# L2 pooling on one core: two 63 KB input slots and pairwise adds in place of four 32 KB slots and a reduce

## The chip, the cores and the metric

The kernel runs on one core of one Trainium2 chip. The metric is the device time of one execution in microseconds (us). The kernel before takes 395.71 us (median of six runs, 395.51 to 395.85). Times below are medians of several executions of the same kernel; all runs with more than one execution are in the fast state, at full clock.

## The reference, cut to what matters

```python
x = randn(32, 256, 4096)  # float32, 134 MB
window = np.abs(x[:, :, 4*i:4*i+4]) ** 2.0          # p == 2, kernel_size == 4
result[:, :, i] = np.mean(window, axis=-1) ** 0.5   # (32, 256, 1024), 34 MB
```

Each input element is read once, squared, summed in fours, and a root is taken of each sum. The data is 33.5 million elements, 262144 for each of the 128 partitions. Nothing is used twice, so 167.8 MB must go through the DMA engines in any version.

## The kernel before

Four input slots of 8192 elements (32 KB) per partition. Three loads are always asked for ahead of the one in use. Four slots make a group with one output tile, which one store sends. ACT (ScalarE) squares in place, DVE (VectorE) reduces in fours, ACT takes the root one chunk later. The last two stores before the final one are held back so that they run while the last load is worked on.

```python
W, CH, GROUP, LAST = 8192, 4096, 4, 1
in_pool  = tile_pool(bufs=4)      # 4 x 32 KB
out_pool = tile_pool(bufs=2)      # 2 x 32 KB
...
for i in range(n):
    if i + 3 < n:
        load(i + 3)                                   # SyncE (SP) queue
    ...
    for c in range(0, W, CH):
        xh = xts[i][:, c:c + CH]
        nc.scalar.activation(out=xh, in_=xh, func=Square)                     # L108
        nc.vector.tensor_reduce(out=ots[gi][:, at:at + CH // k],              # L112
            in_=xh.rearrange("p (n j) -> p n j", j=k), axis=X, op=add)
        if pending is not None:
            root(*pending)        # Sqrt on ACT, L87; store on the ACT queue when a group is done
        pending = (i, c)
root(*pending)
for gi in sorted(held):
    nc.sync.dma_start(out=out_block(gi), in_=ots[gi])
```

## Time and profile before

| | before |
|---|---|
| time, us | 395.71 |
| span of the profiled run, us | 393.7 |
| DVE busy | 72% |
| ACT busy | 75% |
| moved | 167.79 MB, 426 GB/s over the span |

These lines are from the profile page of the kernel before. First the busy share of each engine; then the span in 40 equal slices, with the DMA engines' busy share in tenths and the rate in GB/s; then the packets; then the chain of waits that ended last; then groups of instructions (busy us, mean ns of one | idle before them and what ended it).

```profile
span 393.7 us, 357 instructions
...
DVE 282.8 (72%) x64; ACT 294.7 (75%) x130; POOL 0.2 (0%) x4
...
DMA  8999998999999999999999999999999999999997
GB/s 350 446 430 426 426 426 373 449 446 430 433 426 426 426 430 453 440 430 433 426 426 426 426 449 443 427 433 430 426 426 426 443 446 433 430 433 426 426 435 314
DMA packets 5906, 167.79 MB, mean 426 GB/s; under 512 B 656, under 2 KB 656, under 8 KB 656
...
DMA 72%; ACT 17%; DVE 9%; SPq 0%; issue 0%; ACTq 0%
...
L112 DVE TENSOR_REDUCE ot<-xt 128x1024 f32<-128x4096 f32 x64 | 282.8, 4420 | 103.4 <-ACT xt L108 102.6
L108 ACT ACTIVATE xt<-xt 128x4096 f32<-128x4096 f32 x64 | 230.9, 3610 | 87.6 <-DMA xt<-in_x_dram 85.0
```

The DMA row is full and both compute engines sit idle for about a quarter of the time, so the DMA engines bound the kernel.

The trace also holds every DMA packet with its start and duration. A packet here is one descriptor: one contiguous piece for one partition. Median durations are 309 ns for 8 KB, 912 ns for 24 KB and 1213 ns for 32 KB, which is about 0.03675 ns per byte plus 9 ns.

### The profile page before, as it was taken

What the parts mean: (1) busy time and instruction counts of PE and PEld (TensorE: products, weight loads), DVE (VectorE), ACT (ScalarE), POOL (GpSimd) and SP (SyncE); (2) the same over time, 40 slices, a digit from 0 to 9 for tenths busy, and PEclk for the clock granted to TensorE, in tenths of its full rate; (3) what the DMA queues carried; (4) which work ended last, traced back from release to release, by engine and by line L of the source; (5) the groups of instructions that cost most, each with busy time, mean ns of one, the idle gap of its engine ahead of it and who ended that gap; (6) DMA issues with size and microseconds to landing.
All of it is one profiled execution on the core that took longest, in us unless ns stands there. A gap on an engine that the chain in (4) does not pass through costs nothing.

```text
span 393.7 us, 357 instructions
## 1 busy us (share of the span) xinstructions
DVE 282.8 (72%) x64; ACT 294.7 (75%) x130; POOL 0.2 (0%) x4
## 2 busy tenths in 40 slices
DVE  0399996739976399764988559866598846999992
ACT  1699987469883798828988189863998819999981
POOL 0000000000000000000000000000000000000000
DMA  8999998999999999999999999999999999999997
GB/s 350 446 430 426 426 426 373 449 446 430 433 426 426 426 430 453 440 430 433 426 426 426 426 449 443 427 433 430 426 426 426 443 446 433 430 433 426 426 435 314
DMA packets 5906, 167.79 MB, mean 426 GB/s; under 512 B 656, under 2 KB 656, under 8 KB 656
## 3 DMA queue, kind: packets, MB, share of 16 engines
q1 hardware_dynamic: 4896, 141.56, 83.9%
q10 hardware_dynamic: 1008, 26.21, 15.5%
q14 instruction: 2, 0.02, 0.0%
HBM read 134.22 MB, written 33.55 MB: 426 GB/s over the span
## 4 chain that ended last, share of the span: by engine, by line
DMA 72%; ACT 17%; DVE 9%; SPq 0%; issue 0%; ACTq 0%
DMA xt<-in_x_dram 72%; ACT xt L108 14%; DVE ot L112 9%; ACT ot L87 2%; SPq L79 0%; ACTq L108 0%
## 5 line engine op out<-in xcount | busy, mean ns | idle before, releaser
L112 DVE TENSOR_REDUCE ot<-xt 128x1024 f32<-128x4096 f32 x64 | 282.8, 4420 | 103.4 <-ACT xt L108 102.6
L108 ACT ACTIVATE xt<-xt 128x4096 f32<-128x4096 f32 x64 | 230.9, 3610 | 87.6 <-DMA xt<-in_x_dram 85.0
L87 ACT ACTIVATE ot<-ot 128x1024 f32<-128x1024 f32 x64 | 67.0, 1047 | 4.2 <-DVE ot L112 3.4
L108 ACT ACT_TABLE_LOAD x1 | 1.3, 1283 | 0.7 <-PEq L139 0.7
L87 ACT ACT_TABLE_LOAD x1 | 1.3, 1283 | 0.0
L139 POOL MEMSET const-uint8-127<- 128x1 uint8 x1 | 0.1, 102 | 0.0
L139 POOL MEMSET const-bfloat16-1.0<- 128x1 bf16 x1 | 0.1, 101 | 0.0
L139 POOL MEMSET const-float32-0.0<- 128x1 f32 x1 | 0.1, 98 | 0.2 <-issue 0.2
L139 POOL MEMSET const-float32-1.0<- 128x1 f32 x1 | 0.1, 98 | 0.0
## 6 DMA issues: line engine op xcount, KB each, us to landing
xt<-in_x_dram SPq DMA_DIRECT2D x32, 4096.0 KB, 35.9
out_dram<-ot ACTq DMA_DIRECT2D x6, 4096.0 KB, 23.2
out_dram<-ot SPq DMA_DIRECT2D x1, 4096.0 KB, 34.1
out_dram<-ot SPq DMA_DIRECT2D x1, 3072.0 KB, 12.3
out_dram<-ot ACTq DMA_DIRECT2D x1, 1024.0 KB, 5.6
```

The source lines that it names most:

```text
L87: nc.scalar.activation(out=o, in_=o, func=mybir.ActivationFunctionType.Sqrt, scale=1.0 / k,)
L108: nc.scalar.activation(out=xh, in_=xh, func=mybir.ActivationFunctionType.Square,)
L112: nc.vector.tensor_reduce(out=ots[gi][:, at:at + CH // k], in_=xh.rearrange("p (n j) -> p n j", j=k), axis=mybir.AxisListType.X, op=mybir. ...
L139: nc = _bacc.Bacc("TRN2", target_bir_lowering=False, num_devices=1)
```

## The change

The intent is to give DMA larger descriptors (63 KB instead of 32 KB per partition), with two slots instead of four (126 KB in place of 128 KB), and to shorten the arithmetic so that two slots suffice: two pairwise adds in place of the reduce, and DVE takes an eighth of the squares from ACT. A tail of four loads of 31.5 KB and one of 16 KB per partition ends the kernel.

```diff
-    W = 8192
-    CH = 4096
-    GROUP = 4
+    CH = 4032
+    W = 4 * CH            # 63 KB
+    H = W // 2
+    BIG = 14
+    END = total - BIG * W - 4 * H      # 4096
-    in_pool = ... bufs=4 ; out_pool = ... bufs=2 ; last_pool = ... bufs=1
+    x_pool = ... bufs=2  ; o_pool = ... bufs=2   ; s_pool = ... bufs=2
...
+    def add1(v):          # first adds, L70: columns 0,1 plus 2,3 of each four
+        vv = v.rearrange("p (n j) -> p n j", j=4)
+        nc.vector.tensor_tensor(out=s..., in0=vv[:, :, 0:2], in1=vv[:, :, 2:4], op=Alu.add)
+    def add2(o, s):       # second adds, L78
+        sv = s.rearrange("p (n j) -> p n j", j=2)
+        nc.vector.tensor_tensor(out=o, in0=sv[:, :, 0], in1=sv[:, :, 1], op=Alu.add)
...
+    for i in range(BIG):
+        square_dve(c[3][:, 0:CH // 2])                        # L61
+        square_act(c[0]); square_act(c[1]); square_act(c[2])  # L58
+        square_act(c[3][:, CH // 2:CH])
+        s0 = add1(c[0]); add2(o[0], s0)
+        s1 = add1(c[1]); add2(o[1], s1)
+        s2 = add1(c[2]); s3 = add1(c[3]); add2(o[2], s2); add2(o[3], s3)
+        if i + 2 < BIG:        load(i + 2)                    # L85, SP queue
+        elif i + 2 == BIG:     load_tail((0, 1))              # L103
+        else:                  load_tail((2, 3))
+        root(ot[:, base:base + 2 * CH // k]); root(...)       # L64
+        if i % 2 == 1 and i < BIG - 1:
+            nc.scalar.dma_start(out=block(of, ...), in_=ot)   # L140, ACT queue
...
+    for j in range(5):
+        if j == 2:
+            last_x = load_tail((4,))      # takes the slot of small loads 0 and 1
+        ... per chunk: square_act, add1, add2, root of the chunk before
+    nc.sync.dma_start(..., in_=ot_pair)   # L165, 4.1 MB, held back
+    nc.sync.dma_start(..., in_=ot_three)  # L166, 3.1 MB
+    nc.sync.dma_start(..., in_=ot_two)    # L167, 1.56 MB
```

(The repeated cuts are marked; calls on one line are separate lines in the kernel.)

More of the change, by code (lines that the diff above doesn't have):

```diff
@@ L33 @@
     fp32 = mybir.dt.float32
+    Act = mybir.ActivationFunctionType
+    Alu = mybir.AluOpType
     xf = x.rearrange("b c l -> (b c l)")
@@ L36 @@
     total = xf.shape[0] // P
-    W = 8192
-    CH = 4096
-    GROUP = 4
-    LAST = 1
-    n = total // W
-    assert n * W == total
-    groups = []
-    i = 0
-    while i < n - LAST:
-        g = min(GROUP, n - LAST - i)
-        groups.append((i, g))
-        i += g
-    groups += [(j, 1) for j in range(n - LAST, n)]
-    held = {len(groups) - 1 - LAST - j for j in range(2)}
-    group_of = {}
-    for gi, (first, g) in enumerate(groups):
-        for j in range(g):
-            group_of[first + j] = gi
@@ L59 @@
-    in_pool = ctx.enter_context(tc.tile_pool(name="in_pool", bufs=4))
-    out_pool = ctx.enter_context(tc.tile_pool(name="out_pool", bufs=2))
-    last_pool = ctx.enter_context(tc.tile_pool(name="last_pool", bufs=1))
-    ctx.enter_context(tc.manual_schedule())
-    def x_block(i):
-        first, g = groups[group_of[i]]
-        block = xf[first * W * P:(first + g) * W * P].rearrange("(p w) -> p w", p=P)
-        return block[:, (i - first) * W:(i - first + 1) * W]
-    def out_block(gi):
-        first, g = groups[gi]
-        return of[first * W * P // k:(first + g) * W * P // k].rearrange("(p w) -> p w", p=P)
+    CH = 4032
@@ new lines, with block, square_act @@
+    W = 4 * CH
+    H = W // 2
+    BIG = 14
+    END = total - BIG * W - 4 * H
+    assert END == 4096
+    x_pool = ctx.enter_context(tc.tile_pool(name="x_pool", bufs=2))
+    o_pool = ctx.enter_context(tc.tile_pool(name="o_pool", bufs=2))
+    s_pool = ctx.enter_context(tc.tile_pool(name="s_pool", bufs=2))
+    ctx.enter_context(tc.manual_schedule())
+    def block(flat, first, width):
+        return flat[first * P:(first + width) * P].rearrange("(p w) -> p w", p=P)
+    def square_act(v):
+        nc.scalar.activation(out=v, in_=v, func=Act.Square)
@@ new lines, in square_dve, with root @@
+    def square_dve(v):
+        nc.vector.tensor_tensor(out=v, in0=v, in1=v, op=Alu.mult)
+    def root(o):
+        nc.scalar.activation(out=o, in_=o, func=Act.Sqrt, scale=1.0 / k)
+    def add1(v):
+        s = s_pool.tile([P, CH // 2], fp32, name="s")
+        n = v.shape[1]
+        vv = v.rearrange("p (n j) -> p n j", j=4)
+        nc.vector.tensor_tensor(
+            out=s[:, 0:n // 2].rearrange("p (n j) -> p n j", j=2),
+            in0=vv[:, :, 0:2], in1=vv[:, :, 2:4], op=Alu.add,
+        )
+        return s[:, 0:n // 2]
@@ L74 @@
+    def add2(o, s):
+        sv = s.rearrange("p (n j) -> p n j", j=2)
+        nc.vector.tensor_tensor(out=o, in0=sv[:, :, 0], in1=sv[:, :, 1], op=Alu.add)
     xts = {}
-    ots = {}
     def load(i):
-        xt = in_pool.tile([P, W], fp32)
-        nc.sync.dma_start(out=xt, in_=x_block(i))
+        xt = x_pool.tile([P, W], fp32, name="xt")
+        nc.sync.dma_start(
+            out=xt, in_=block(xf, i // 2 * 2 * W, 2 * W)[:, i % 2 * W:(i % 2 + 1) * W],
+        )
         xts[i] = xt
-    def root(i, c):
-        first, g = groups[group_of[i]]
-        ot = ots[group_of[i]]
-        at = ((i - first) * W + c) // k
-        o = ot[:, at:at + CH // k]
-        nc.scalar.activation(
-            out=o, in_=o, func=mybir.ActivationFunctionType.Sqrt, scale=1.0 / k,
-        )
-        if i == first + g - 1 and c + CH == W and group_of[i] not in held:
-            nc.scalar.dma_start(out=out_block(group_of[i]), in_=ot)
@@ L93 @@
-    for i in range(3):
-        load(i)
-    pending = None
-    for i in range(n):
-        if i + 3 < n:
-            load(i + 3)
-        gi = group_of[i]
-        first, g = groups[gi]
-        if i == first:
-            pool = last_pool if i >= n - LAST else out_pool
-            ot = pool.tile([P, g * W // k], fp32)
-            ots[gi] = ot
-        for c in range(0, W, CH):
-            xh = xts[i][:, c:c + CH]
-            nc.scalar.activation(
-                out=xh, in_=xh, func=mybir.ActivationFunctionType.Square,
-            )
-            at = ((i - first) * W + c) // k
-            nc.vector.tensor_reduce(
-                out=ots[gi][:, at:at + CH // k],
-                in_=xh.rearrange("p (n j) -> p n j", j=k),
-                axis=mybir.AxisListType.X, op=mybir.AluOpType.add,
-            )
-            if pending is not None:
-                root(*pending)
-            pending = (i, c)
@@ L120, with load_tail @@
-    root(*pending)
-    for gi in sorted(held):
-        nc.sync.dma_start(out=out_block(gi), in_=ots[gi])
+    tail_at = BIG * W
+    tail = [(tail_at + j * H, H) for j in range(4)] + [(tail_at + 4 * H, END)]
+    three = block(xf, tail_at, 3 * H)
+    two = block(xf, tail_at + 3 * H, H + END)
+    tail_src = [three[:, 0:H], three[:, H:2 * H], three[:, 2 * H:3 * H], two[:, 0:H], two[:, H:]]
+    tail_x = {}
+    def load_tail(js):
+        xt = x_pool.tile([P, W], fp32, name="xt")
+        at = 0
+        for j in js:
+            w = tail[j][1]
+            nc.sync.dma_start(out=xt[:, at:at + w], in_=tail_src[j])
+            tail_x[j] = xt[:, at:at + w]
+            at += w
+        return xt
@@ new lines @@
+    load(0)
+    load(1)
+    ot = None
+    for i in range(BIG):
+        xt = xts[i]
+        if i % 2 == 0:
+            ot = o_pool.tile([P, 2 * W // k], fp32, name="ot")
+        base = i % 2 * W // k
+        c = [xt[:, j * CH:(j + 1) * CH] for j in range(4)]
+        o = [ot[:, base + j * CH // k:base + (j + 1) * CH // k] for j in range(4)]
+        square_dve(c[3][:, 0:CH // 2])
+        square_act(c[0])
+        square_act(c[1])
+        square_act(c[2])
+        square_act(c[3][:, CH // 2:CH])
+        s0 = add1(c[0])
+        add2(o[0], s0)
+        s1 = add1(c[1])
+        add2(o[1], s1)
+        s2 = add1(c[2])
+        s3 = add1(c[3])
+        add2(o[2], s2)
+        add2(o[3], s3)
+        if i + 2 < BIG:
+            load(i + 2)
+        elif i + 2 == BIG:
+            load_tail((0, 1))
+        else:
+            load_tail((2, 3))
+        root(ot[:, base:base + 2 * CH // k])
+        root(ot[:, base + 2 * CH // k:base + W // k])
+        if i % 2 == 1 and i < BIG - 1:
+            nc.scalar.dma_start(out=block(of, (i - 1) * W // k, 2 * W // k), in_=ot)
@@ new lines @@
+    ot_pair = ot
+    ot_three = o_pool.tile([P, 2 * W // k], fp32, name="ot")
+    ot_two = None
+    pending = None
+    for j in range(5):
+        if j == 2:
+            last_x = load_tail((4,))
+            ot_two = last_x[:, END:END + (H + END) // k]
+        w = tail[j][1]
+        step = CH if w == H else w // 2
+        for c in range(0, w, step):
+            v = tail_x[j][:, c:c + step]
+            square_act(v)
+            s = add1(v)
+            at = (j * H + c) // k if j < 3 else ((j - 3) * H + c) // k
+            o = (ot_three if j < 3 else ot_two)[:, at:at + step // k]
+            add2(o, s)
+            if pending is not None:
+                root(pending)
+            pending = o
@@ L126 @@
+    root(pending)
+    nc.sync.dma_start(out=block(of, (BIG - 2) * W // k, 2 * W // k), in_=ot_pair)
+    nc.sync.dma_start(out=block(of, tail_at // k, 3 * H // k), in_=ot_three[:, 0:3 * H // k])
+    nc.sync.dma_start(out=block(of, (tail_at + 3 * H) // k, (H + END) // k), in_=ot_two)
 _INS = ['x', 'p', 'kernel_size']
```

## The prediction

> **What bounds it now.** The DMA engines. The page's DMA row is 8s and 9s throughout: 167.79 MB in a span of 393.7 us (426 GB/s), with DVE 72% and ACT 75% busy. The chain that ended last is 72% DMA. In the trace's DMA packet records all 16 engines are occupied without a break from 1.9 to about 391 us, so no wait between engines costs anything. Only bytes (unchanged), cost per descriptor, the head and the end can move the time.
>
> **Cost per descriptor.** Median packet times are 309 ns (8 KB), 912 ns (24 KB) and 1213 ns (32 KB): 0.0368 ns/B plus about 9 ns. The slope is 435 GB/s over 16 engines, which agrees with the fabric ceiling in the Trainium skill (DMA: Bandwidth & Descriptors, "Where 436 GB/s comes from"). Per engine there are now 256 load and 72 store descriptors (328); afterwards 152 + 72 = 224. Estimated gain: 104 x 9 ns = 0.9 us, plus 0.1 us for 13 fewer completion writes.
>
> **Compute per 63 KB slot** (estimates). ACT from the trace is (n+236)/1.2 ns (3610 ns for 4096, 1047 for 1024): three squares of 4032 at 3.56 us, one of 2016 at 1.88, two roots at 1.87: 16.3 us. No tensor_tensor is in this trace; the skill (VectorE: DVE Perf Modes, the errata section) gives (N+151)/0.96 ns for an fp32 one, and the reduce's 4420 ns for 4096 fits about the same form. So a 2016-wide op is 2.26 us and a 1008-wide one 1.21: five and four of them are 16.1 us. Two adds (3.46 us) replace a 4.36 us reduce.
>
> **Two slots.** A slot is read about 15.3 us after it lands (ACT squares, then the last first-adds); the next load can be moving 1 us later. Meanwhile the other slot's load takes 19.0 us, more when a 4.1 MB store (9.5 us) shares it. So the queue should not run dry in the 14 large loads, but the reserve is only about 2.5 us: with DVE 10% slower a gap of about 1 us appears, with 20% about 4 us.
>
> **The end.** Here it loses. ACT has about 10 us of work in hand when the tail starts and then needs 4.6 us per 4032 chunk, about the DMA's pace, so it never catches up. The fifth small load waits for the second one's adds (DMA gap 0.5 to 2 us). ACT finishes its last root about 64 us after the last large load lands; the held stores are over by then, so DMA idles about 3.7 us before the last 1.56 MB store. Before, there is no such gap: the 1 MB store ran beside the end of the 3 MB one.
>
> **Sum.** 395.7 - 1.0 + about 0.7 + about 2.6 (the last gap, less overlaps) = 398 us. Range 395 to 402. Faster by over 2%: 0.02; within 2%: 0.88; slower by over 2%: 0.10.
>
> **What would show it.** Load packets near 2380 ns; DMA row full until about 360 us, then a short gap before the fifth small load and one of 3 to 4 us before the last store; first-adds at 2.26 us, second at 1.21; in the chain that ended last, mostly ACT after the last large load.
>
> **What would make it wrong.** Strided two-input adds slower than one element per cycle (steady gaps, 402 us and more); 63 KB descriptors cut up or moved at another rate; stores sharing the engines unequally with the larger load descriptors; held stores covering the last computation better than I count (then about 395).

## More of the kernel before

The windows view gives the rate over a long stretch more exactly. Its columns are: the stretch, its length, busy us of DVE, ACT and POOL, the granted clock, the DMA share and GB/s.

```profile
68.00:330.00 262.00, 186.46 (x43) 192.46 (x86) 0.00 (x0) 1.00 1.00 433
```

So 433 GB/s is what the sixteen DMA engines move here when little disturbs them. (This view counts a packet where it starts, so the rate of a short stretch can be off by one or two per cent.)

## The result, and the profile after

| | before | after |
|---|---|---|
| median, us | 395.71 | 401.21 |
| range of six runs, us | 395.51 to 395.85 | 399.89 to 403.12 |
| span of the profiled run, us | 393.7 | 400.1 |

The ratio is 1.0143, 95% interval 1.0117 to 1.0169. Ratios here are the mean time of one kernel's fast runs over that of the other's fast runs of the same rounds, so not quite the ratio of the medians quoted. The kernel is slower by 1.4%, and its runs scatter ten times as widely as before. The predicted time was 398.0.

The same lines of the profile page after the change:

```profile
span 400.1 us, 388 instructions
...
DVE 252.1 (63%) x146; ACT 265.3 (66%) x106; POOL 0.2 (0%) x4
...
DMA  9999999999999999999999999999999999998995
GB/s 380 439 419 413 413 471 368 451 451 426 413 416 461 458 420 413 439 416 448 439 417 393 455 445 432 393 426 432 439 458 384 435 419 429 422 451 344 375 426 245
DMA packets 4034, 167.79 MB, mean 419 GB/s; under 512 B 448, under 2 KB 448, under 8 KB 448
...
DMA 55%; DVE 22%; ACT 16%; issue 5%; DVEq 0%; ACTq 0%
...
L70 DVE TENSOR_TENSOR s<-xt 128x2016 f32<-128x2016 f32 (+1 forms) x66 | 145.7, 2226 | 31.1 <-ACT xt L58 31.1
L61 DVE TENSOR_TENSOR xt<-xt 128x2016 f32<-128x2016 f32 x14 | 31.6, 2258 | 106.8 <-DMA xt<-in_x_dram 106.8
L78 DVE TENSOR_TENSOR ot<-s 128x1008 f32<-128x1008 f32 x62 | 73.6, 1205 | 1.2
```

Both compute engines are less busy than before (63% and 66%). The bytes are the same, the packets a third fewer. The DMA row is even fuller in the first 36 slices. And yet the rate is lower: 419 GB/s against 426. This is the first thing to learn here: **a DMA engine that is busy is not an engine that moves data at full rate.** The windows view of the kernel after, for the stretch shown above and for 18 us near the end, and then the same 18 us of the kernel before:

```profile
68.00:330.00 262.00, 168.08 (x97) 168.24 (x65) 0.00 (x0) 1.00 1.00 429
...
362.00:380.00 18.00, 14.32 (x9) 18.00 (x9) 0.00 (x0) 1.00 0.94 360
...
362.00:380.00 18.00, 16.25 (x5) 16.82 (x9) 0.00 (x0) 1.00 1.01 437
```

In the loop the DMA share is 1.00, as before, but the rate is 429, not 433. In the tail a stretch of 18 us moves only 360 GB/s, where the kernel before moves 437.

To see more than the views give, I counted the DMA packet records. *Slow* is the time by which packets last longer than 0.03675 ns per byte plus 9 ns, summed and divided by 16 engines. *Idle* is engine time with no packet in flight, divided by 16. Both are in us:

```
profiled run       ideal   loop 68-330     362-380        from 380       last packet
                   sum     slow   idle     slow  idle     slow  idle     ends
before             388.2   0.31   0.10     0.04  0.00     0.21  0.70     392.5
after              387.3   2.47   0.07     1.85  1.30     0.03  2.51     398.8
```

The ideal sum fell by 0.9 us, as predicted; the medians are 2380 ns for the 63 KB packets. Against that stand slow and idle together, 2.1 us more in the loop, 3.1 us more between 362 and 380 us, and 1.6 us more at the end. Together with the 0.9 us gained that is 5.9 us, against 6.4 us by which the spans of the two profiled runs differ. (The profiled run after took 401.93 us, the second longest of the six, so these terms are those of one of the longer runs. The slow packets of the loop are all packets of loads: one of them lasted 1.0 us too long, and no packet of the stores beside them more than 0.002 us.)

The chain of waits shows what the tail is made of. These are its pieces around the last large load and at the end (start us, duration, what):

```profile
297.00 33.32 DMA xt<-in_x_dram
330.35 3.57 ACT xt L58
...
366.27 3.45 ACT xt L58
369.72 0.93 ACT ot L64
370.66 3.45 ACT xt L58
374.11 0.93 ACT ot L64
...
391.31 0.63 ACT xt L64
```

From 330.35 us, where ACT is released by the last large load (its last packet ended at 328.8), to 391.94 us, where the last root ends, the tail takes 61.6 us. ACT is the limiter there for much of it: one square and one root per chunk, 4.39 us. The DMA issues of SP in this stretch, from the timeline:

```profile
367.65 0.33 SPq L103 DMA_DIRECT2D xt<-in_x_dram  x1
...
368.03 0.42 SPq L165 DMA_DIRECT2D out_dram<-ot  x1
...
391.97 0.33 SPq L167 DMA_DIRECT2D out_dram<-xt  x1
```

The fifth small load is issued at 367.65 us. Its first packet starts at 368.6 us. In the packet records the engines end the loads before it between 367 and 369.3 us, so most of them had run dry by then. Its 16 KB packets then last 842 ns on average where 611 is their undisturbed time.

### The profile page after: what moved, and what is told of

Its sections match the earlier page's. It is cut to its first block, busy times and chain, and to the rows that moved or that the text cites. A ratio compares the mean times of both kernels' runs of the same rounds, so it can differ in the third digit from the quotient of the medians.

```text
span 400.1 us, 388 instructions
## 1 busy us (share of the span) xinstructions
DVE 252.1 (63%) x146; ACT 265.3 (66%) x106; POOL 0.2 (0%) x4
## 4 chain that ended last, share of the span: by engine, by line
DMA 55%; DVE 22%; ACT 16%; issue 5%; DVEq 0%; ACTq 0%
DMA xt<-in_x_dram 55%; DVE s L70 15%; ACT xt L58 13%; DVE ot L78 6%; ACT ot L64 2%; DVE xt L78 0%; ACT xt L64 0%; DVEq L70 0%; ACTq L64 0%
## 5 line engine op out<-in xcount | busy, mean ns | idle before, releaser
L58 ACT ACTIVATE xt<-xt 128x4032 f32<-128x4032 f32 (+1 forms) x66 | 203.5, 3144 | 80.3 <-DMA xt<-in_x_dram 79.8
L70 DVE TENSOR_TENSOR s<-xt 128x2016 f32<-128x2016 f32 (+1 forms) x66 | 145.7, 2226 | 31.1 <-ACT xt L58 31.1
L61 DVE TENSOR_TENSOR xt<-xt 128x2016 f32<-128x2016 f32 x14 | 31.6, 2258 | 106.8 <-DMA xt<-in_x_dram 106.8
L64 ACT ACTIVATE ot<-ot 128x2016 f32<-128x2016 f32 (+1 forms) x34 | 58.7, 1726 | 43.3 <-DVE ot L78 43.2
L78 DVE TENSOR_TENSOR ot<-s 128x1008 f32<-128x1008 f32 x62 | 73.6, 1205 | 1.2
L64 ACT ACTIVATE xt<-xt 128x1008 f32<-128x1008 f32 (+1 forms) x4 | 3.3, 828 | 2.3 <-DVE xt L78 2.3
L78 DVE TENSOR_TENSOR xt<-s 128x1008 f32<-128x1008 f32 (+1 forms) x4 | 3.8, 950 | 0.1
```

The lines of the kernel that those rows point to most:

```text
L58: nc.scalar.activation(out=v, in_=v, func=Act.Square)
L61: nc.vector.tensor_tensor(out=v, in0=v, in1=v, op=Alu.mult)
L64: nc.scalar.activation(out=o, in_=o, func=Act.Sqrt, scale=1.0 / k)
L70: nc.vector.tensor_tensor(out=s[:, 0:n // 2].rearrange("p (n j) -> p n j", j=2), in0=vv[:, :, 0:2], in1=vv[:, :, 2:4], op=Alu.add,)
L78: nc.vector.tensor_tensor(out=o, in0=sv[:, :, 0], in1=sv[:, :, 1], op=Alu.add)
```

## The experiments

The theories, as the expectations name them:

- **A**, thin reserve: with two slots, the next load is asked for only 15 us after a landing, so the queue of load descriptors is short, and that costs time in the loop.
- **B**, descriptor size: 63 KB packets are slow beside stores.
- **C**, two queues: stores on ACT's queue share the DMA engines with the load on SP's queue, and the switch costs time.
- **T**, the tail: the late fifth small load, and ACT's tail.

Of these runs stores_late, read_short and two_desc_short give wrong results. All times, with the ratio to the kernel before of the same rounds (there 395.45 to 395.72 us):

| run | median, us | range, us | ratio (95% interval) |
|---|---|---|---|
| compute_only | 397.37 | 397.30 to 397.40 | 1.0045 (1.0030 to 1.0060) |
| two_desc | 402.59 | 399.63 to 404.31 | 1.0191 (1.0153 to 1.0230) |
| stores_late | 399.68 | 398.80 to 400.17 | 1.0101 (1.0085 to 1.0117) |
| read_short | 399.07 | 398.49 to 399.74 | 1.0088 (1.0073 to 1.0104) |
| t4_early | 400.55 | 400.05 to 400.94 | 1.0119 (1.0102 to 1.0136) |
| tail_both | 400.98 | 400.67 to 401.63 | 1.0136 (1.0121 to 1.0151) |
| store_sp | 396.59 | 396.42 to 396.73 | 1.0023 (1.0008 to 1.0038) |
| three_slot | 396.61 | 396.57 to 396.88 | 1.0025 (1.0010 to 1.0040) |
| two_desc_short | 397.42 | 396.90 to 398.30 | 1.0046 (1.0033 to 1.0060) |
| two_slot_42 | 416.29 | 414.83 to 417.88 | 1.0522 (1.0492 to 1.0551) |
| three_slot_b | 395.64 | 395.51 to 395.71 | 0.9998 (0.9986 to 1.0011) |
| two_slot_mended | 396.81 | 396.74 to 397.20 | 1.0032 (1.0016 to 1.0047) |
| last_sp | 398.71 | 398.21 to 399.72 | 1.0081 (1.0063 to 1.0099) |
| two_desc_b | 403.91 | one run | none |
| three_slot_c | 395.72 | 395.55 to 395.85 | 1.0004 (0.9991 to 1.0016) |
| three_slot_sp | 396.30 | 395.98 to 396.74 | 1.0021 (1.0008 to 1.0033) |

And the same count of packet records for the runs with two 63 KB slots:

```
profiled run       loop 68-330     362-380        from 380
                   slow   idle     slow  idle     slow  idle
after              2.47   0.07     1.85  1.30     0.03  2.51
read_short         2.67   0.08     1.90  0.26     0.02  0.86
two_desc           0.76   0.08     1.78  1.87     0.04  0.61   its fastest run
two_desc_b         3.76   0.33     1.98  2.29     0.03  0.55   one of its long runs
two_desc_short     0.38   0.08     1.09  0.05     0.03  0.98
t4_early           3.42   0.07     0.17  0.00     0.04  3.62
tail_both          3.12   0.14     0.20  0.01     0.06  3.85
store_sp           1.64   0.09     0.05  0.00     0.01  1.87
last_sp            2.85   0.10     0.01  0.00     0.01  2.40
two_slot_mended    1.02   0.08     0.06  0.02     0.01  2.44
```

### compute_only: the new arithmetic in the old slots

```diff
 # kernel before
-nc.scalar.activation(xh, Square); nc.vector.tensor_reduce(...)
+if c == 0: nc.vector.tensor_tensor(v, v, v, mult)   # an eighth of the slot
+nc.scalar.activation(rest of the chunk, Square)
+for half in range(2): add1 into s (4 KB); add2
```

> The kernel before with its four 32 KB slots, its loads, stores and tail, but the new arithmetic: VectorE squares an eighth of each slot and sums in pairwise adds (in two halves per chunk, for lack of memory). If the arithmetic costs nothing because the DMA engines bound the kernel: 395.7 us within 0.5. If the new arithmetic is itself a cause of the loss: 398 us or more.

The time was 397.37 us, 1.7 us above before and outside the half us that I allowed. The packet records put it at the end: in the loop the slow time is 0.38 us, against 0.31 before, and the idle time from 380 us on is 2.6 us against 0.7. So the arithmetic costs next to nothing in the loop. At the end the last chunk's sums arrive later, in my version with four adds in a row per chunk, and the last store is issued at 388.19 us instead of 387.26. But its packets begin only 0.2 us later than before, and of the 2.6 us of idle only 0.2 lie before 391.5 us. The rest is an uneven end: one engine works alone for the last 1.5 us, until 394.3 (before: for 0.5 us, until 392.5). So most of the 1.7 us is a late engine, which the expectation did not foresee and which no run explains; the arithmetic is cleared for the loop, not for the end.

### two_desc, read_short, two_desc_short: descriptor size and reserve, alone and together

two_desc takes quarters 0 and 2 (or 1 and 3) of the block in one DMA, so that each partition needs two descriptors of 31.5 KB:

```diff
-nc.sync.dma_start(out=xt, in_=block(...)[:, i % 2 * W:(i % 2 + 1) * W])
+nc.sync.dma_start(out=xt.rearrange("p (a w) -> p a w", a=2),
+    in_=block(...).rearrange("p (a b w) -> p a b w", a=2, b=2)[:, :, i % 2, :])
```

> The changed kernel with the same two 63 KB slots, but each load fetches two separate pieces of 31.5 KB per partition, so two descriptors per partition in one DMA; the arithmetic is unchanged and the result right. Theory A (the loss in the middle comes from the thin reserve of two slots, the next load being asked for late): 401 us plus about 1 us for 112 more descriptors per engine. Theory B (large descriptors, interleaved with the stores, cost the time): the slow packets after each store's start vanish and the time falls to 399 us or less.

read_short leaves out the square and the first add of a slot's third chunk, so that a slot is free earlier:

```diff
-square_act(c[2])
-s1 = add1(c[1]); add2(o[1], s1)
-s2 = add1(c[2])
+s1 = add1(c[1])
 s3 = add1(c[3])
-add2(o[2], s2)
+add2(o[1], s1); add2(o[2], s3)
```

> The changed kernel without the square and the adds of a slot's third chunk in the 14 large slots (wrong result on purpose): the slot is read about 3.5 us earlier after its landing, DMA traffic is the same. Theory A (thin reserve): the slow packets of every second load vanish, the last large load lands about 2 to 3 us earlier and the time falls by 3 us or more, to 398 us or less. Theories B and C (descriptor size, queue switch): slow packets stay at each store's start, and the time falls only by what the tail gains.

two_desc_short has both edits.

> Two descriptors of 31.5 KB per partition and load, as in two_desc, and the slot read 3.5 us earlier, as in read_short (wrong result on purpose). two_desc alone was unsteady (399.6 to 404.3 us) though its profiled run lost only 0.8 us to slow packets in the middle. If that unsteadiness is the thin reserve, this run is steady, within 1 us, and with the middle's slow packets gone it is about 2 us below read_short: 397 us. If packet size has no part in it, it stays at 399 us.

two_desc was no faster (402.59 us; by its ratio the record calls it unclear at 2%), against theory B, but its profiled run, the fastest of the four, had lost only 0.76 us in the loop. read_short gained 2.1 us (399.07 against 401.21), but its slow packets in the loop were all there, 2.67 us, against theory A; what it gained came after the loop: 1.0 us at the fifth small load, which met engines less dry, and 1.6 us at the end, most of it because no engine was as late there as in the changed kernel (see the last experiments). Either theory alone fails. Together the edits do nearly what was expected of them: 397.42 us, 0.38 us of slow packets in the loop, and a range of 1.4 us, not the 1 us that was asked for but far less than two_desc's 4.7. Since read_short and two_desc_short differ only in the descriptors, 63 KB cost there 1.7 us (399.07 - 397.42), even though they save about 1 us of per-descriptor time. The descriptors of a load also set how it shares the engines with a store, which I did not separate: in the changed kernel 64 load packets and 64 store packets start between 72 and 86 us, one for one, so a store beside the 63 KB packets takes 25 to 27 us, and in two_desc, beside packets of 31.5 KB, 19 to 20 us, while the first load beside a store takes 30.3 us instead of 27.8 and lands later. And two_desc and two_desc_short differ only in how early a slot is free (and in the backlog of the tail), which points to the thin reserve as what made two_desc unsteady.

> The kernel of two_desc again, one look. If it falls among its slow runs (401 to 404 us), the profile shows where: by the theory of the thin reserve, slow packets and gaps at the boundaries of the large loads, above the 0.8 us of its fast run. If it falls among the fast ones (below 400.5 us) it tells nothing new.

This was one of the long runs, 403.91 us; its clock is 1.00 and it lies within the range of two_desc's timed runs. Here are three stretches of the windows view, each around the start of a store beside a large load. First the short run, then the long one, of the same program:

```profile
196.00:215.00 19.00, 15.30 (x9) 15.40 (x7) 0.00 (x0) 1.00 1.00 428
248.00:262.00 14.00, 10.29 (x7) 10.40 (x5) 0.00 (x0) 1.00 1.01 429
298.00:312.00 14.00, 10.26 (x7) 12.47 (x5) 0.00 (x0) 1.00 1.01 433
```

```profile
196.00:215.00 19.00, 15.30 (x9) 15.40 (x7) 0.00 (x0) 1.00 0.99 396
248.00:262.00 14.00, 10.29 (x7) 10.39 (x4) 0.00 (x0) 1.00 1.00 399
298.00:312.00 14.00, 10.30 (x7) 10.40 (x5) 0.00 (x0) 1.00 1.00 392
```

The DMA share is full in both, and the long run moves 7 to 9% less in these stretches (6 to 9% when each packet is shared out by time). They were chosen where its loss lies; from 68 to 330 us it moves 427 GB/s against 432. So in one and the same program, with a thin reserve, the loss comes and goes from run to run. That the scatter of the changed kernel is the same thing is likely, but only one of its runs has a profile.

### two_slot_42 and three_slot: the number of slots

three_slot is a new version with the same arithmetic, three slots of 42 KB (W = 4 * 2688), 24 large loads, one last load of 16 KB, and stores of three slots on ACT's queue; two stores are held for the end. two_slot_42 is the same with two slots, but for its last held store, which is cut in two as in three_slot_b below:

```diff
-x_pool bufs=3 ... for i in range(3): load(i) ... load(i + 3)
+x_pool bufs=2 ... for i in range(2): load(i) ... load(i + 2)
```

> A version meant to beat both: the new arithmetic in three slots of 42 KB (24 loads of 42 KB per partition, one last load of 16 KB), three pieces per store, two stores of 4.1 MB held back to cover the last computation. The reserve is two loads, about 14 us. If thin reserve and tail were the causes: no slow packets after the first store's start, 0.5 us less for 56 fewer descriptors per engine, 395.0 to 395.6 us. If large descriptors are themselves slow beside stores: about 1 us of slow packets in the middle, 396 us or more.

> three_slot with two slots instead of three, all else equal: loads of 42 KB per partition, stores on ScalarE's queue. It asks whether it is the number of slots, thus how many load descriptors are queued when a store starts, or the descriptor's size that makes packets slow in the middle. If the number of slots: slow packets of 2 us or more return, plus run-dry gaps, since the reserve is only about 1 us: 399 us or more. If the size of 63 KB is the cause: the middle stays below 0.5 us of slow packets, and the time is near three_slot's 396.6, but for gaps.

One slot fewer costs 19.7 us (416.29 against 396.61), or 20.7 us against three_slot_b (395.64), which differs from two_slot_42 in nothing else. In two_slot_42 the loop shows 9.7 us of slow packets and 2.6 us of idle; three_slot shows 0.23 and 0.11, and its window has the full rate of the kernel before:

```profile
68.00:330.00 262.00, 172.87 (x145) 174.89 (x98) 0.00 (x0) 1.00 1.00 433
```

So the reserve decides here: with an estimated 1 us of it 42 KB descriptors do badly, with a whole extra load they do well. In these runs a thin reserve shows far more as packets that last longer than as gaps. The layout in memory is not the cause: a partition's piece of a block is 126 KB long in three_slot as in the changed kernel. The time of three_slot missed its expectation (395.0 to 395.6) because of a gap at the end; see below.

### t4_early and tail_both: the tail

```diff
-if j == 2: last_x = load_tail((4,))
+if j == 1:                                  # half slot that small load 0 has left
+    tail_x[4] = first_x[:, 0:END]
+    nc.sync.dma_start(out=tail_x[4], in_=tail_src[4])
```

tail_both adds to this:

```diff
-square_act(v)
+square_dve(v[:, 0:step // 6]); square_act(v[:, step // 6:])
```

> The changed kernel, but the fifth small load goes into the half slot that the first small load has left, so it waits for the first small load's adds, not for the second's, and is queued about 9 us earlier, while others are in flight. Theory T (the tail's DMA gap and the slow restart of that load, together 3 us, delay everything after): those 3 us vanish from the stretch 362 to 380 us. But ScalarE's chain of squares and roots is unchanged, so if it is the second limit of the tail the last root still ends near 392 us, the gap before the last store grows to 3 us or more and the time falls only by about 2 us, to 399. If ScalarE is no limit: 398 us or less.

> The fifth small load early as in the other run, and VectorE squares a sixth of every tail chunk, which takes 0.55 us off ScalarE per chunk of 4032 and so about 5 us off its tail. If both limits of the tail are named rightly, 396.5 to 398 us: only the loss in the middle (2.5 us) is left, less 1 us for fewer descriptors. If the tail is not what costs: above 399.5 us.

In t4_early the loss of 3.15 us between 362 and 380 us was gone, as the windows view shows, and so was the slowness of the 16 KB packets:

```profile
362.00:380.00 18.00, 14.18 (x9) 18.00 (x10) 0.00 (x0) 1.00 1.01 430
```

But the time fell by only 0.7 us. That is within the scatter of the changed kernel. The last store was issued at 393.13 us, later than the 391.97 us of the kernel after. The chain of computation was as long as ever: 61.6 us from ACT's first square of the last large load (331.51 us) to the end of the last root. And it began 1.2 us later; this run's loop lost 3.42 us to slow packets, 0.95 more than that of the profiled run after. The DMA engines, now done earlier, waited: the idle time from 380 us on rose from 2.51 to 3.62 us. So the tail has two limits of nearly equal length, and removing one hands the time to the other.

tail_both was to remove both and gained nothing (400.98). Its timeline shows why. On DVE the first-adds (L70) begin at 352.89, 357.26, 361.64 and 366.01 us, 4.37 us apart: with 0.78 us of squares added, DVE paces the tail exactly as ACT had, at 4.39 us. I gave away too much: a sixth of the squares made the other engine the limit.

### stores_late, store_sp, last_sp: where the stores stand in line

stores_late sends all the stores behind the last load. store_sp issues the six stores on SP's queue, where they come after the next load. last_sp does so with the last of them only.

```diff
 # store_sp; in last_sp only for i == BIG - 3
-nc.scalar.dma_start(out=block(of, (i - 1) * W // k, 2 * W // k), in_=ot)
+nc.sync.dma_start(out=block(of, (i - 1) * W // k, 2 * W // k), in_=ot)
```

> The changed kernel with its six stores in the loop moved behind the last load (wrong result on purpose: they all send the last pair's output). Same bytes, no store runs beside a load. Theory A (thin reserve): every load, not only every second one, now has a reserve of about 3 us, so slow packets or gaps show at every load boundary, in sum 3 us or more over the 14 loads. Theory C (the switch between the load and the store queue costs the time): packets are 2380 ns throughout and the middle loses nothing. The gap before the last store vanishes under each theory, so the time falls: A 398 to 400 us, C 396 us.

> The changed kernel with its six stores issued on SyncE's queue, behind the next load, instead of on ScalarE's: no round robin between two queues, all in one order. Theory C (the switch between queues makes the slow packets at each store's start): they vanish, 2 us faster, 399 us. Theory B (large load descriptors beside or next to a store, in whichever queue): slow packets stay; the time stays near 401 us.

> The changed kernel with only the last of the six loop stores on SyncE's queue, behind the last large load; the other five stay on ScalarE's. If the loss was that the last large load shared the engines with a store and so landed late, in front of a tail that ScalarE bounds: that load lands about 7 us earlier relative to what is left to move, and most of store_sp's gain comes: 397 to 398 us. If it is the sharing throughout the loop: at most a sixth of the gain, 400 us or more.

stores_late took 399.68 us. Without any store beside a load, the 14 loads still lost 1.7 us to slow packets and 0.7 us to gaps, so sharing with stores is not their only cause. It lies between the expectations of A and C; the fifth small load still met a dry queue there and lost 3.3 us.

store_sp took 396.59 us: 4.6 of the 5.5 us are recovered, with the same slots, descriptors and arithmetic. The loop's slow packets fell less than expected, to 1.64 us. The larger part comes at the end. When two queues had work, the engines alternated between them (the 64 and 64 packets above), and so the last large load shared them with the sixth store: by the packet records the load landed at 328.8 us and the store ended at 331.2. In one queue the load goes first and lands at 320.6 us; the store, which nobody waits for, ends at 328.8. The whole chain of the tail then starts 8 us earlier relative to what is left to move, and the fifth small load is asked for before the engines run dry: no loss at all between 362 and 380 us. The end of store_sp in the timeline:

```profile
385.12 0.63 ACT L64 ACTIVATE xt<-xt 128x512 f32<-128x512 f32 x1 [1.50 <-DVE xt L78]
385.78 0.33 SPq L167 DMA_DIRECT2D out_dram<-xt  x1
```

The last root ends at 385.75 us instead of 391.94. last_sp measures this part alone: 398.71 us, 2.5 us recovered, about half of the 4.6, and the time lies between the two ranges expected; the load landed at 323.1 us and the loss between 362 and 380 us was 0.01 us. The five stores that stayed on ACT's queue kept the loop's slow packets at 2.85 us. The order at the end is thus worth about 2.5 us, and keeping the other stores in line about 2.1 us more (398.71 - 396.59). Whether these 2.1 us come from not sharing, or from the longer queue that stores in the same line make, no run separates.

### two_slot_mended, three_slot_b, three_slot_c, three_slot_sp: a version that beats both?

two_slot_mended joins store_sp, t4_early and a twelfth of the tail's squares on DVE.

> The changed kernel with three repairs: stores on SyncE's queue behind the next load (store_sp), the fifth small load into the first's half slot (t4_early), and VectorE squares a twelfth of the tail's chunks, which keeps both engines near 4.1 us per chunk. store_sp left 1.9 us of DMA gap at the end; if that is ScalarE's tail, it vanishes: 394.7 to 395.2 us, level with or just below the kernel before. What is left then are the slow packets of the middle, 1.6 us.

three_slot_b cuts three_slot's last held store in two; three_slot_c also moves the last small load's first square in front of the last group's last root; three_slot_sp has all stores on SP's queue.

```diff
 # three_slot_b
-held.append((dst, ot))
+held.append((dst[:, 0:cut], ot[:, 0:cut])); held.append((dst[:, cut:], ot[:, cut:]))   # cut: two of three slots
 # three_slot_c
+if i == BIG - 1: square_act(xts[BIG][:, 0:END // 2])     # between the two roots
```

> three_slot had a DMA gap of 2.6 us near 380 us, since the last held store waited for the roots of the whole last group. Here that store is cut in two, two thirds (6.3 us of DMA) not waiting for the last slot. If that gap was all that kept it above the kernel before, it goes and the time falls by about 2.5 us to 394.1 us, 0.4% below before. If the tail is bound by something else it stays above 395.5 us.

> three_slot_b with the first square of the last small load put in front of the last root of the last group, in ScalarE's wait of 2.3 us. The last store should start about 1.5 to 2 us earlier and the last DMA gap of 1.7 us shrink to below 0.7: 394.6 us, 0.25% below the kernel before. If it stays at 395.6, the end is bound by the slowest DMA engine, not by ScalarE.

> three_slot_c with all stores on SyncE's queue behind the next load. Every kernel with stores on ScalarE's queue lost 0.6 to 1.1 us of slow packets near 58 us, at its first store; store_sp lost 0.1 us there. If that is the cost of the second queue's first use: 0.6 us less than three_slot_c, 394.0 us. If one queue brings other losses (a store waiting at the head of the queue delays the loads behind it): the same as three_slot_c or more.

None beats the kernel before. three_slot_b equals it: 395.64 us, ratio 0.9998. three_slot's gap near 380 us, 2.65 us of idle, is closed, but the time fell by 1.0 us, not 2.5. three_slot_c computed its last output 1.6 us earlier and gained nothing, and two_slot_mended finished its last root at 384.69 us, 1.1 us before store_sp, and was no faster either (396.81 us; 394.7 to 395.2 was expected). The packet records show what is in the way: the engines do not finish together. In the changed kernel fifteen engines are through with the last store by 396.6 us; one goes on until 398.8. In two_slot_mended one or two engines work alone for the last 2 us, in three_slot_b and three_slot_c one or two for the last 1.5 us or so; in the kernel before it is one for 0.5 us. Why one engine falls behind is open.

three_slot_sp tested the loss of 0.6 to 1.1 us that kernels with a store in the loop show at their first store. It did not go, it moved: 0.81 us at 76 us, where the first store runs there. So it goes with the first store, not with the first use of ACT's queue. And three_slot_sp was slower than three_slot_c, 396.30 us against 395.72, with ranges that do not touch; in the loop after 90 us it lost 0.4 us to slow packets against 0.2. With three slots, then, stores in the loads' queue gained nothing.

## Why the prediction was right or wrong

The direction, the class and the range were right: slower, within 2%, and 401.2 lies between 395 and 402. The size was wrong: 2.3 us slower was forecast, 5.5 us came.

- **"The DMA engines" bound the kernel.** Right. compute_only, with different arithmetic, leaves the loop untouched (0.38 us of slow packets against 0.31).
- **Descriptors, gain of 0.9 + 0.1 us.** Right: 2380 ns per packet, 224 data descriptors per engine, ideal sum 388.2 to 387.3 us. The 0.1 us for fewer completion writes was not measured alone. The slope of 0.03675 ns per byte on 16 engines is 435 GB/s, the fabric ceiling in the Trainium skill (DMA: Bandwidth & Descriptors, "Where 436 GB/s comes from").
- **Compute.** Right: 2.26 us and 1.21 us for the adds in the timeline, 2.258 us for DVE's square. The formula for an fp32 tensor_tensor add in the Trainium skill (VectorE: DVE Perf Modes, the section on the errata), (N+151)/0.96 ns, gives estimates of 2257 and 1207 ns. So the strided operands cost nothing that shows.
- **"So the queue should not run dry in the 14 large loads."** This is the first step that failed. The queue did not run dry, 0.07 us idle, but I took "not dry" for "at full rate". The loop lost 2.1 us more than before, nearly all of it in slow packets, with the DMA share at 1.00. Estimated at 0, measured 2.1. With two slots, two_desc_short shows, it takes both a wider reserve and smaller load descriptors to be rid of it; three slots of 42 KB are rid of it too.
- **"DMA gap 0.5 to 2 us" at the fifth small load.** The gap was 1.3 us, within that; but the load that starts on dry engines is itself slow, 1.85 us more. The term of 0.7 in the sum measured 3.1.
- **"About 2.6" for the last gap.** The mechanism is real: t4_early shows it at nearly the predicted size, with the idle time from 380 us at 3.6 us. In the changed kernel itself the DMA engines came to the end too late to wait: what is lost there is 1.6 us above before, and most of it is the one late engine, which I had not foreseen. That 1.6 came out near 2.6 is luck: it is another loss.
- **"Stores sharing the engines unequally"** stood among the things that would make the prediction wrong, and belonged in the sum. I counted a store beside a load as an increase of the reserve ("more when a 4.1 MB store shares it"). It also delays the very load that the computation waits for. At the last large load that is worth 2.5 us (last_sp), and over all stores 4.6 us (store_sp).

So the sum was -1.0 + 0 + 0.7 + 2.6 = 2.3, and it should have read -0.9 + 2.1 + 3.1 + 1.6 = 5.9 for the profiled runs, which differ by 6.4 in span. These terms are a count of where the engines lost time, not of what each repair gains: t4_early removed 3.1 us of them and gained 0.7.

What stays open: by what mechanism packets become slow when few load descriptors are queued, in particular with 63 KB each, and why one DMA engine ends behind the others. No run here looks inside a DMA engine.

## What to carry to other kernels

In this kernel, which DMA bounds, larger descriptors were worth only their count times 9 ns. Do not pay for that with queue depth: with a short reserve the rate fell before any gap showed (429 GB/s at a DMA share of 1.00), and it fell differently from run to run. Read the GB/s next to the DMA share. With two slots, it paid to keep a store that nobody waits for behind the load that everybody waits for: in the same queue it went after, in another queue it went beside and made the load late, and about half of the gain lay at the last load, before a tail that computation bounds. With three slots the same move gained nothing.

## What the Trainium skill lacked or had wrong

- DMA: Bandwidth & Descriptors, "Issuing engines are not separate DMA queues", says that issuing DMAs on several engines "will only save the time on the sequencer". That they interleave agrees with these traces (64 load and 64 store packets between 72 and 86 us), but the choice of the queue also sets the order in which loads and stores share the engines: moving six stores from ACT's queue to SP's gained 4.6 us of 401.2, and the last large load landed 8.2 us earlier. With three slots it gained nothing (396.30 us against 395.72).
- The same page's rule for maximum bandwidth ("128 partitions, ≥1 MiB per DMA") is met by every load here, and rates in the windows shown still differed from 360 to 437 GB/s. It lacks the queue's reserve: 42 KB descriptors with three slots lost 0.3 us in the loop, with two slots 12.3 us.
- I found no page that says that a DMA engine's packets can last longer, with hardly a gap, in a kernel that asks for its loads late: 2.5 us in the loop at a DMA share of 1.00, and 9.7 us in two_slot_42.
- I found no page with the cost of the first store after loads alone: about 0.4 to 1.1 us of slow packets in the kernels here with stores in their loop, on either queue (two_slot_42 apart, where it cannot be told from the other slow packets).
- The DMA page, "Why a DMA increments its semaphore by 16 and not by 1", says that the engines of one DMA finish independently. It gives no size; here the last store ended on one engine 2.2 us after the other fifteen.
